# A two-block fp32 kernel: the weights' low halves leave GpSimd, three branch products move in front of the mLSTM norms, a wide norm takes its bank from the product banks

## The chip, the cores and the metric

The kernel runs on one core of one Trainium2 chip. The time is the device time of one execution in microseconds (us). Three runs of the kernel before took 1544.9, 1547.41 and 1548.17 us; their median is 1547.41 us. The engines are named as in the profile: PE does matmuls (PEld its weight loads), DVE is the vector engine, ACT the scalar engine, POOL GpSimd, and SP issues most of the DMAs. Each engine works through its own instructions in their order.

## The reference, cut to what matters

Two transformer-like blocks follow each other over 512 positions of width 1024, all in float32. The first adds 16 meta tokens, so it works on 528 positions.

```
first block
  h = rmsnorm(x);  proj = h @ w_in  -> u, q, k, v, o, gates, ga, gb
  y_a = gelu(ssm(u)) * sigmoid(... @ w_glu)                 # state space branch
  hb  = mlstm(q, k, v, gates)                                # 4 heads of 128
  y_b = hb * rsqrt(mean(hb*hb)) * g_head * sigmoid(o)        # a norm for each head
  merged = sigmoid(ga) * (y_a @ w_a) + sigmoid(gb) * (y_b @ w_b)
  x = x + rmsnorm(merged @ w_out)                            # "post norm"
  x = x + rmsnorm((gelu(conv(h @ w_gate)) * (h @ w_up)) @ w_down)
second block
  x = x + (four head groups A, B, C, D, each its own attention, group norm) @ w_out_2
  x = x + cross_attention(x, 256 memory tokens)
  x = x + relu(h @ w_up_2)**2 @ w_down_2
  return rmsnorm(x)
```

## The kernel before, in words

Activations lie with features on the 128 partitions and positions along the free dimension. To reach float32 accuracy every operand of a product is split in two: a high half (the value rounded to PE's fast float32 form) and a low half (what is left). A product is then three matmuls for each block of 128 features: high by high, high by low, low by high (`mm3`, lines 130 to 138; `product`, lines 150 to 175).

Weights come through `weights` (lines 112 to 128): a DMA by SP into a staging tile `wst`, a cast to the high half `whi` (line 125 on ACT, or line 123 on DVE), and a subtraction for the low half `wlo` (line 126). Each of the three tiles has three buffers. The engine of line 126 is `self.wlow`. It is DVE in most of the kernel. It is POOL from the time that the second block's attention begins until the end of the cross attention (set around the `weave` in `hybrid`, and in `cross`). While it is POOL, every second high half is cast on DVE instead of ACT.

The accumulation banks come from pools. `product_bank` (lines 177 to 189) hands out a bank for a product: where a pool `pmx` of three more banks is open, `mm` (two buffers) and `mx` (three) take turns; where it is not and `third` is set, every third product uses the single bank `rs`; otherwise only the two `mm` banks are used. The row norms use the bank `rs`: `rstd_wide` (lines 249 to 266) sums squares with a matmul by ones (line 257), takes Ln and Exp on ACT (lines 260, 261) and refines on DVE (lines 263 to 266; line 264 is the last to read the bank). `rstd_steps` uses `rs` twice, for column sums (line 279) and for spreading the result (line 294).

The stages that the change touches, in order of time in the trace:

- the end of the mLSTM, about 330 to 350 us: the last head's units, then Ln and Exp of the row scales `rows` on ACT (lines 853 and 854, each with a table load), then matmuls by an identity column that spread `rows` over partitions (line 858, bank `st`), a multiply (line 861) and the split of y_b.
- the merge, about 338 to 400 us: `branch(f, 0)` multiplies y_a by its weights and `branch(f, 1)` y_b by its own; f runs over 8 blocks. The first three `branch(f, 0)` stand first in the code, behind the mLSTM norms.
- the output product and the post norms, about 400 to 475 us: 8 products for each of two halves of the positions, then `post_norm` for each half. The second half's norm runs beside the products of memory keys and values (`memory_keys`, lines 1565 to 1608) and the first products of the feed forward part. No `pmx` is open there, so these products share the two `mm` banks.
- the attention of the second block, about 865 to 1100 us: softmax or stick-breaking steps of one head (DVE, ACT, POOL, PE in turns) woven with the projections of the next.
- the cross attention, about 1100 to 1200 us.

The order of the instructions on each engine is not that of the code: a scheduler reorders the program with a model of its own. So a change of engines also moves instructions.

Of the kernel before, what the change touches and what calls it, by code (L numbers as in the profile page):

```python
# [11 lines left out]
FT = mybir.dt.float32  # L12
FR = mybir.dt.float32r
AF = mybir.ActivationFunctionType
OP = mybir.AluOpType
# [4 lines left out]
P = 128  # L20
DM = 1024
KT = DM // P
# [3 lines left out]
T0 = NM - 2  # L26
# [37 lines left out]
class Net:  # L64
    def __init__(self, ctx, tc, I, out, dump=None):
# [13 lines left out]
        self.wlow, self.turns = nc.vector, 0  # L79
# [32 lines left out]
    def weights(self, src, shape, own=None):  # L112

        nc = self.nc
        kt, cols = shape
        n = kt * cols
        st = self.wst.tile([P, 1024], FT, name="wst")
        nc.sync.dma_start(st[:, 0:n] if len(src.shape) == 2 else st[:, 0:n].rearrange("p (k c) -> p k c", k=src.shape[1]),
                          src)
        hi, lo = ((own or self.whi).tile([P, 1024], FR, name="whi"), (own or self.wlo).tile([P, 1024], FR, name="wlo"))  # L120
        self.turns += 1
        if self.wlow is nc.gpsimd and self.turns % 2:
            nc.vector.tensor_copy(hi[:, 0:n], st[:, 0:n])
        else:
            nc.scalar.activation(hi[:, 0:n], st[:, 0:n], AF.Copy)  # L125
        self.wlow.tensor_tensor(lo[:, 0:n], st[:, 0:n], hi[:, 0:n].bitcast(FT), OP.subtract)  # L126
        v = lambda t: t[:, 0:n].rearrange("p (k c) -> p k c", k=kt)
        return v(hi), v(lo)
# [120 lines left out]
    def rstd_wide(self, out, accs, t, width=DM, bank=None):  # L249
# [6 lines left out]
        for j, acc in enumerate(accs):  # L256
            mm = nc.tensor.matmul(ps, self.ones, acc, start=j == 0, stop=j == len(accs) - 1)
            if bank is not None and j == 0:
                self.tc.keep_in_program_order(mm)
# [447 lines left out]
    def mixer(self):  # L707
# [3 lines left out]
        with ExitStack() as es:  # L711
# [23 lines left out]
            with ExitStack() as e2:  # L735
# [4 lines left out]
                with tc.tile_pool(name="tmp0", bufs=1, side="right", reuse_waits="tile") as tmp:  # L740
# [33 lines left out]
                    for (t0, n) in FULL:  # L774
                        known = self.rstd_wide(rs[:, t0:t0 + n], [a[:, t0:t0 + n] for a in self.nacc],
                                               tmp.tile([P, 264], FT, name=f"rw{t0}"),
                                               bank=self.ptr.tile([P, 512], FT, name="tr"))
# [33 lines left out]
            with ExitStack() as e2:  # L811
# [40 lines left out]
                row = self.rows[:, T0:L]  # L852
                nc.scalar.activation(row, row, AF.Ln, scale=1.0 / P)
                nc.scalar.activation(row, row, AF.Exp, scale=-0.5)
                for h in range(4):
# [13 lines left out]
            jobs = self.merge(self.pool(es, "memp"), mt, yas, ybs, sga, gb, sgs, a2, b2)  # L869
# [36 lines left out]
    def merge(self, mem, mt, yas, ybs, sga, gb, sgs, a2, b2):  # L906
# [3 lines left out]
        mg = []  # L910
# [3 lines left out]
        def branch(f, i):  # L914

            if f not in ws:
                ws[f] = self.weights(I["w_ab"][f], (8, P))
# [3 lines left out]
            for (t0, n) in TAIL:  # L921
# [9 lines left out]
        for f, i in [(0, 0), (1, 0), (2, 0), (0, 1)] + [  # L931
                fi for f in range(1, KT) for fi in ((f, 1), (f + 2, 0)) if fi[0] < KT]:
            branch(f, i)
# [8 lines left out]
        for i, (t0, n) in enumerate(TAIL):  # L942
# [10 lines left out]
            steps = self.post_norm(mt, [y[:, t0 - T0:t0 - T0 + n] for y in yo], accs, t0, n, "g_ffn_pre")  # L953
# [52 lines left out]
    def post_norm(self, pool, ys, accs, t0, n, gnext):  # L1006
# [3 lines left out]
        self.rstd_wide(pr, accs, pool.tile([P, 258], FT, name="prt"))  # L1010
# [298 lines left out]
    def hybrid(self):  # L1309
# [3 lines left out]
        with ExitStack() as es:  # L1313
# [221 lines left out]
            self.wlow = nc.gpsimd  # L1535
            self.vx = self.pool(e2, "vx", 1)
            self.weave([(heads(*hs), expand(jobs)) for hs, jobs in plan[1:]])
            self.wlow = V
# [79 lines left out]
    def cross(self, es, out):  # L1618
# [13 lines left out]
        self.wlow = nc.gpsimd  # L1632
# [95 lines left out]
        self.wlow = V  # L1728
# [213 lines left out]
```

## Time and profile before

| what | value |
|---|---|
| median of three runs | 1547.41 us |
| the profiled execution | 1552.2 us, its span 1550.5 us |
| PE busy | 1474.9 us (95%) |
| DVE busy | 1027.4 us (66%) |
| ACT busy | 728.2 us (47%) |
| POOL busy | 329.9 us (21%) |
| mean granted TensorE clock | 0.989 |

The span runs from the first to the last instruction. A matmul's row shows when it started and a modelled end; matmuls overlap. The idle time of PE is what a change on the other engines can win. In the rows below, a bracket such as [1.69 <-DVE ptl L107] says that the engine stood idle for 1.69 us before this instruction and that a DVE instruction of line 107 ended the wait.

### The profile page before, as it was taken

To read this page: it belongs to the slowest core of one execution; us is meant where nothing else is said; L and a number is where in the kernel's file an instruction comes from. 1 tells how busy PE (TensorE), PEld (TensorE's weight loads), DVE (VectorE), ACT (ScalarE), POOL (GpSimd) and SP (SyncE) were. 2 spreads that over 40 slices of the span, in tenths; PEclk is the share of its full clock that TensorE was granted. 3 is DMA by queue.
4 is the path that set the end of the run, shared out by engine and by line. 5 is a ranking of instruction groups with operands and counts; after the bars stand their busy time and mean duration, and the time that the engine had idled before them with its cause. 6 is when DMAs were issued, how large, how long until landed. Compare 5 with 4: busy or idle time off the path is not lost.

```text
span 1550.5 us, 25022 instructions
## 1 busy us (share of the span) xinstructions
PE 1474.9 (95%) x9769; PEld 1326.8 (86%) x9769; DVE 1027.4 (66%) x1946; ACT 728.2 (47%) x1420; POOL 329.9 (21%) x304
## 2 busy tenths in 40 slices
PE   7999899989989999999999999989789999999996
PEld 7899899879988899999999877878788888888886
DVE  6988889777587555555476778888886443344334
ACT  5323356664655333334454556575565431134322
POOL 1157821003341000000142354303432000000001
PEclk9999999999999999999999999999999999999999
DMA  6333332226553232324656122114221233333221
GB/s 204 98 110 94 111 105 77 73 96 194 161 157 116 96 93 92 91 94 139 187 170 199 55 68 69 48 41 144 84 67 42 95 96 95 95 96 95 92 85 55
DMA packets 66431, 161.97 MB, mean 104 GB/s; under 512 B 15100, under 2 KB 24556, under 8 KB 66184
## 3 DMA queue, kind: packets, MB, share of 16 engines
q1 hardware_dynamic: 64936, 157.74, 33.0%
q8 instruction: 77, 1.26, 0.3%
q0 software_dynamic: 288, 1.57, 0.3%
q10 hardware_dynamic: 1088, 1.05, 0.2%
q14 instruction: 42, 0.34, 0.1%
HBM read 153.92 MB, written 10.33 MB: 106 GB/s over the span
## 4 chain that ended last, share of the span: by engine, by line
PE 55%; DVE 10%; ACT 3%; issue 1%; POOL 0%; ACTq 0%; DVEq 0%; POOLq 0%
PE mm L135 6%; PE mm L138 6%; PE mm L136 6%; PE mm L165 5%; PE mm L168 5%; PE mm L167 5%; PE mx L165 4%; PE mx L168 4%; PE mx L167 4%; DVE xl L110 2%; PE mx L135 2%; PE mx L138 2%; PE mx L136 2%; DVE ptl L107 1%; PE tr L1219 1%
## 5 line engine op out<-in xcount | busy, mean ns | idle before, releaser
L126 DVE TENSOR_TENSOR wlo<-wst,whi 128x1024 fp32r<-128x1024 f32 (+2 forms) x227 | 284.4, 1254 | 200.0 <-ACT whi L125 121.5
L125 ACT ACTIVATE whi<-wst 128x1024 fp32r<-128x1024 f32 (+3 forms) x244 | 251.9, 1033 | 290.0 <-PE mm L136 107.5
L167 PE MATMUL mm<-xh,whi 128*128 128x256 f32 (+4 forms) x792 | 228.7, 314 | 2.5 <-DVE u L751 2.3
L168 PE MATMUL mm<-xl,whi 128*128 128x256 f32 (+4 forms) x792 | 229.3, 314 | 0.3 <-DVE xl L110 0.3
L167 PE MATMUL mx<-xh,whi 128*128 128x512 f32 (+3 forms) x584 | 176.5, 324 | 7.5 <-ACT xh L109 6.8
L168 PE MATMUL mx<-xl,whi 128*128 128x512 f32 (+3 forms) x584 | 177.6, 326 | 3.3 <-DVE xl L110 3.2
L167 PEld LDWEIGHTS mm<-xh,whi 128*128 128x128 f32 (+1 forms) x792 | 149.8, 189 | 12.9 <-DVE u L751 2.6
L168 PEld LDWEIGHTS mm<-xl,whi 128*128 128x128 f32 (+1 forms) x792 | 149.7, 189 | 10.6 <-issue 0.6
L135 PE MATMUL mm<-hh,whi 128*128 128x256 f32 (+1 forms) x496 | 139.9, 311 | 0.0
L136 PE MATMUL mm<-hl,whi 128*128 128x256 f32 (+1 forms) x496 | 139.7, 311 | 0.0
L165 PE MATMUL mm<-xh,wlo 128*128 128x256 f32 (+4 forms) x792 | 137.6, 313 | 0.0
L167 PEld LDWEIGHTS mx<-xh,whi 128*128 128x128 f32 x584 | 110.5, 189 | 16.7 <-ACT xh L109 7.1
L165 PEld LDWEIGHTS mm<-xh,wlo 128*128 128x128 f32 (+1 forms) x792 | 114.6, 188 | 10.3 <-issue 0.4
L168 PEld LDWEIGHTS mx<-xl,whi 128*128 128x128 f32 x584 | 110.3, 189 | 14.3 <-DVE xl L110 5.0
L165 PE MATMUL mx<-xh,wlo 128*128 128x512 f32 (+3 forms) x584 | 105.9, 322 | 0.0
L126 POOL TENSOR_TENSOR wlo<-wst,whi 128x1024 fp32r<-128x1024 f32 (+1 forms) x34 | 75.2, 2215 | 124.1 <-PE mm L138 39.8
L135 PEld LDWEIGHTS mm<-hh,whi 128*128 128x128 f32 x496 | 93.5, 189 | 6.2
L136 PEld LDWEIGHTS mm<-hl,whi 128*128 128x128 f32 x496 | 93.6, 189 | 5.8
L1004 POOL TENSOR_TENSOR acc<-acc,osq 128x256 f32<-128x256 f32 (+1 forms) x26 | 24.8, 954 | 345.4 <-ACT osq L1001 345.3
L165 PEld LDWEIGHTS mx<-xh,wlo 128*128 128x128 f32 x584 | 87.1, 187 | 9.1
L138 PE MATMUL mm<-hh,wlo 128*128 128x256 f32 (+1 forms) x496 | 83.9, 310 | 1.3 <-DVE wlo L126 1.3
L138 PEld LDWEIGHTS mm<-hh,wlo 128*128 128x128 f32 x496 | 70.8, 189 | 7.4 <-DVE wlo L126 1.7
(555 smaller groups left out, 3317.3 us busy)
## 6 DMA issues: line engine op xcount, KB each, us to landing
wst<-in_w_in_dram SPq DMA_DIRECT2D x52, 512.0 KB, 3.5
wst<-in_w_down_dram SPq DMA_DIRECT2D x32, 512.0 KB, 3.5
wst<-in_w_mup_dram SPq DMA_DIRECT2D x32, 512.0 KB, 3.5
wst<-in_w_mdown_dram SPq DMA_DIRECT2D x32, 512.0 KB, 3.8
wst<-in_w_gate_dram SPq DMA_DIRECT2D x22, 512.0 KB, 3.5
wst<-in_w_up_dram SPq DMA_DIRECT2D x22, 512.0 KB, 3.5
wst<-in_w_out_dram SPq DMA_DIRECT2D x20, 512.0 KB, 3.6
wst<-in_w_down_dram SPq DMA_DIRECT2D x16, 384.0 KB, 3.6
```

Of the source, the lines that this page charges most:

```text
L107: nc.vector.tensor_tensor(lo, src, hi.bitcast(FT), OP.subtract)
L110: nc.vector.scalar_tensor_tensor(lo, src, gain, hi.bitcast(FT), OP.mult, OP.subtract)
L125: nc.scalar.activation(hi[:, 0:n], st[:, 0:n], AF.Copy)
L126: self.wlow.tensor_tensor(lo[:, 0:n], st[:, 0:n], hi[:, 0:n].bitcast(FT), OP.subtract)
L135: nc.tensor.matmul(ps, ah, bh, start=start and i == 0, stop=False)
L136: nc.tensor.matmul(ps, ah, bl, start=False, stop=False)
L138: nc.tensor.matmul(ps, al, bh, start=False, stop=stop and i == n - 1)
L165: nc.tensor.matmul(ps, wl[:, k], xh, start=False, stop=k == KT - 1)
L167: nc.tensor.matmul(ps, wh[:, k], xh, start=k == 0, stop=False)
L168: nc.tensor.matmul(ps, wh[:, k], xl, start=False, stop=False)
L1004: nc.gpsimd.tensor_tensor(acc, acc, sq, OP.add)
L1219: nc.tensor.matmul(yp[0:64, c0:c1], m[:, j, vc:vc + 64], d[:, j - f0, c0:c1], start=ji == x == 0, stop=ji == len(jobs) - 1 and x == 2)
```

## The change

1. `weights` loses the choice of engine: all high halves are cast by ACT, all low halves are subtracted by DVE, in the attention and the cross attention as elsewhere.
2. `branch` and the loading of its weights become functions of their own, `branches`. The weights of f = 0, 1, 2 and the products `branch(f, 0)` of these three are now written ahead of and behind the Ln and Exp of `rows`, in front of the spreading matmuls, while the mLSTM's own banks are still open and `pmx` is not. So these six products (three f, two ranges) use `mm` and `rs` in turns.
3. `post_norm` in the merge takes its bank from `product_bank` instead of `rs`. That also shifts which of `mm` and `mx` the later products get. A flag `late` keeps the fixed place of the first norm of the program as it was.

```
@@ -76,7 +76,6 @@
         self.nrm = ent("nrm")
         self.dram = ent("dram", 1, DR)
         self.pmx, self.turn, self.third = None, 0, 0
-        self.wlow, self.turns = nc.vector, 0
         self.pmm = ent("pmm", 2, PS)
 
         c = self.const
@@ -118,12 +117,8 @@
         nc.sync.dma_start(st[:, 0:n] if len(src.shape) == 2 else st[:, 0:n].rearrange("p (k c) -> p k c", k=src.shape[1]),
                           src)
         hi, lo = ((own or self.whi).tile([P, 1024], FR, name="whi"), (own or self.wlo).tile([P, 1024], FR, name="wlo"))
-        self.turns += 1
-        if self.wlow is nc.gpsimd and self.turns % 2:
-            nc.vector.tensor_copy(hi[:, 0:n], st[:, 0:n])
-        else:
-            nc.scalar.activation(hi[:, 0:n], st[:, 0:n], AF.Copy)
-        self.wlow.tensor_tensor(lo[:, 0:n], st[:, 0:n], hi[:, 0:n].bitcast(FT), OP.subtract)
+        nc.scalar.activation(hi[:, 0:n], st[:, 0:n], AF.Copy)
+        nc.vector.tensor_tensor(lo[:, 0:n], st[:, 0:n], hi[:, 0:n].bitcast(FT), OP.subtract)
         v = lambda t: t[:, 0:n].rearrange("p (k c) -> p k c", k=kt)
         return v(hi), v(lo)
 
@@ -246,7 +241,7 @@
             pass
         return self.r
 
-    def rstd_wide(self, out, accs, t, width=DM, bank=None):
+    def rstd_wide(self, out, accs, t, width=DM, bank=None, late=False):
 
 
         nc = self.nc
@@ -255,7 +250,7 @@
         ps = (self.pmm.tile([P, 512], FT, name="rs", bufs=1) if bank is None else bank)[:, 0:n]
         for j, acc in enumerate(accs):
             mm = nc.tensor.matmul(ps, self.ones, acc, start=j == 0, stop=j == len(accs) - 1)
-            if bank is not None and j == 0:
+            if late and j == 0:
                 self.tc.keep_in_program_order(mm)
         nc.scalar.activation(out, ps, AF.Ln, scale=1.0 / width, bias=self.eps)
         nc.scalar.activation(out, out, AF.Exp, scale=-0.5)
@@ -774,7 +769,7 @@
                     for (t0, n) in FULL:
                         known = self.rstd_wide(rs[:, t0:t0 + n], [a[:, t0:t0 + n] for a in self.nacc],
                                                tmp.tile([P, 264], FT, name=f"rw{t0}"),
-                                               bank=self.ptr.tile([P, 512], FT, name="tr"))
+                                               bank=self.ptr.tile([P, 512], FT, name="tr"), late=True)
                     for i, piece in enumerate(pieces):
                         if i not in early:
                             piece()
@@ -850,8 +845,15 @@
                 self.weave([(units, fill)])
 
                 row = self.rows[:, T0:L]
+                mg = []
+                load, branch = self.branches(mg, sga, gb, a2, b2)
+                for f in range(3):
+                    load(f)
                 nc.scalar.activation(row, row, AF.Ln, scale=1.0 / P)
                 nc.scalar.activation(row, row, AF.Exp, scale=-0.5)
+
+                for f in range(3):
+                    branch(f, 0)
                 for h in range(4):
                     for (t0, n) in TAIL:
                         ps = self.pst.tile([P, 512], FT, name="st")[:, 0:n]
@@ -866,7 +868,9 @@
                     self.dump("yb", h, ybs[h])
             self.third = 0
             self.pmx = self.pool(es, "pmx2", 3, PS)
-            jobs = self.merge(self.pool(es, "memp"), mt, yas, ybs, sga, gb, sgs, a2, b2)
+            for f, i in [(0, 1)] + [fi for f in range(1, KT) for fi in ((f, 1), (f + 2, 0)) if fi[0] < KT]:
+                branch(f, i)
+            jobs = self.merge(self.pool(es, "memp"), mt, yas, ybs, mg, sgs)
         self.ffn(*jobs)
 
     def pool(self, es, name, bufs=1, space=None, side=None):
@@ -903,18 +907,18 @@
         return pre, [(lambda i=i: load(i), [lambda f=f, r=r: part(f, *r) for f in (2 * i, 2 * i + 1) for r in TAIL])
                      for i in range(2)]
 
-    def merge(self, mem, mt, yas, ybs, sga, gb, sgs, a2, b2):
+    def branches(self, mg, sga, gb, a2, b2):
+
         nc = self.nc
         V = nc.vector
         I = self.I
-        mg = []
         free = [8, 9, 10, 11, 12, 13, 14, 15, 0, 1, 2, 3, 4, 5, 6, 7]
         ws = {}
 
         def branch(f, i):
 
             if f not in ws:
-                ws[f] = self.weights(I["w_ab"][f], (8, P))
+                load(f)
             wh, wl = ws[f]
             if i:
                 mg.append([self.ring.tile([P, L], FR, name=f"r{j}") for j in free[2 * f:2 * f + 2]])
@@ -927,10 +931,14 @@
                 if i:
                     nc.gpsimd.tensor_tensor(gs[0], gs[0], gs[1], OP.add)
                     self.split(mg[f][0][:, t0:t0 + n], mg[f][1][:, t0:t0 + n], gs[0], 0.5)
-
-        for f, i in [(0, 0), (1, 0), (2, 0), (0, 1)] + [
-                fi for f in range(1, KT) for fi in ((f, 1), (f + 2, 0)) if fi[0] < KT]:
-            branch(f, i)
+        def load(f):
+            ws[f] = self.weights(I["w_ab"][f], (8, P))
+        return load, branch
+
+    def merge(self, mem, mt, yas, ybs, mg, sgs):
+        nc = self.nc
+        V = nc.vector
+        I = self.I
         self.xp = self.pool(self.ctx, "xp", side="right")
         self.load_x(self.xp, I["x"], [nc.sync])
         self.bias_rows(mt)
@@ -950,7 +958,8 @@
                 next(steps, None)
             for _ in steps:
                 pass
-            steps = self.post_norm(mt, [y[:, t0 - T0:t0 - T0 + n] for y in yo], accs, t0, n, "g_ffn_pre")
+            steps = self.post_norm(mt, [y[:, t0 - T0:t0 - T0 + n] for y in yo], accs, t0, n, "g_ffn_pre",
+                                   self.product_bank)
 
         e2 = ExitStack()
         jobs = self.ffn_jobs(e2)
@@ -1003,11 +1012,11 @@
                 return [acc, sq]
             nc.gpsimd.tensor_tensor(acc, acc, sq, OP.add)
 
-    def post_norm(self, pool, ys, accs, t0, n, gnext):
+    def post_norm(self, pool, ys, accs, t0, n, gnext, bank=None):
 
         V = self.nc.vector
         pr = pool.tile([P, 258], FT, name="prs")[:, 0:n]
-        self.rstd_wide(pr, accs, pool.tile([P, 258], FT, name="prt"))
+        self.rstd_wide(pr, accs, pool.tile([P, 258], FT, name="prt"), bank=bank and bank())
         yield
         for k in range(KT):
             x = self.x[k][:, t0:t0 + n]
@@ -1532,10 +1541,8 @@
             e3.close()
             self.at = self.pool(e2, "at", 6)
             self.ap = self.pool(e2, "ap", 1)
-            self.wlow = nc.gpsimd
             self.vx = self.pool(e2, "vx", 1)
             self.weave([(heads(*hs), expand(jobs)) for hs, jobs in plan[1:]])
-            self.wlow = V
             if self.dump:
                 for n in range(KT):
                     self.dump("y" + "ABCD"[n // 2], n % 2, ys[n])
...
```

The two left-out places only set `self.wlow` back and forth around the cross attention, as the fragment at line 1532 does for the attention.

How the scheduler then orders the engines is seen at three places. `order` rows name line, operation, and output<-inputs; the numbers behind the names tell tiles of one name apart.

On DVE in the stick-breaking steps of head group B (`pth`, `ptl` are the high and low halves of the score tile `e`; `qkn` is a normalised projection of the next head), before:

```order
L1266 CAST pth0_10695<-e_10649 128x128
L1259 TENSOR_SCALAR e_10703<-tr_10606 128x128
L1267 TENSOR_TENSOR ptl0_10696<-e_10649,pth0_10695 128x128
L1248 SCALAR_TENSOR_TENSOR e_10660<-sc_10657,e_10660 128x384
L123 CAST whi_11293<-wst_11291 128x1024
L107 TENSOR_TENSOR ptl1_10540<-e_10660,pth1_10539 128x384
L1365 SCALAR_TENSOR_TENSOR qkn_10938<-mm_11099,rs_8436 128x512
```

The same place after the change:

```order
L1275 CAST pth0_10695<-e_10649 128x128
L1276 TENSOR_TENSOR ptl0_10696<-e_10649,pth0_10695 128x128
L1257 SCALAR_TENSOR_TENSOR e_10660<-sc_10657,e_10660 128x384
L1374 SCALAR_TENSOR_TENSOR qkn_10938<-mm_11099,rs_8436 128x512
L121 TENSOR_TENSOR wlo_11294<-wst_11291,whi_11293 128x1024
L1257 SCALAR_TENSOR_TENSOR e_10715<-tr_10712,e_10715 128x512
L106 TENSOR_TENSOR ptl1_10540<-e_10660,pth1_10539 128x384
```

The cast of `whi_11293` has gone to ACT. Its low half, which POOL subtracted, stands on DVE as `wlo_11294`, ahead of `ptl1_10540`.

On PE at the end of the mLSTM (the `wlo` rows end a `branch(f, 0)` product; line 858 of before, 860 of after, spreads `rows`), before, where three such products (banks `mm_4505`, `mm_4539`, `mm_4573`) stand ahead of the spreading:

```order
L138 MATMUL mm_4573<-xh0_4180,wlo_4556 128x256
L138 MATMUL mm_4573<-xh1_4182,wlo_4556 128x256
L138 MATMUL mm_4573<-xh2_4184,wlo_4556 128x256
L138 MATMUL mm_4573<-xh3_4186,wlo_4556 128x256
L858 MATMUL st_4432<-rows_104,ident_78 128x258
L858 MATMUL st_4437<-rows_104,ident_78 128x256
```

After:

```order
L131 MATMUL rs_4506<-xl3_4187,whi_4444 128x258
L133 MATMUL rs_4506<-xh0_4180,wlo_4445 128x258
L133 MATMUL rs_4506<-xh1_4182,wlo_4445 128x258
L133 MATMUL rs_4506<-xh2_4184,wlo_4445 128x258
L133 MATMUL rs_4506<-xh3_4186,wlo_4445 128x258
L133 MATMUL mm_4520<-xh3_4186,wlo_4445 128x256
L1118 MATMUL rs_5073<-ya0_5068,rel_5066 12x320
L860 MATMUL st_4534<-rows_104,ident_78 128x258
L860 MATMUL st_4539<-rows_104,ident_78 128x256
```

Six products stand ahead of the spreading now (`mm_4450`, `rs_4464`, `mm_4478`, `mm_4492`, `mm_4520`, `rs_4506`). The three with 258 or 256 columns that have moved came behind the spreading matmuls before.

On PE at the second post norm (line 257 of before, 252 of after, sums the squares; `ya` and `yb` are the high and low halves of the memory tokens; `mm_6007` and `mm_5870` are products of memory values or keys), before:

```order
L138 MATMUL mm_6007<-whi_5918,yb0_5153 128x256 x2
L138 MATMUL mm_6007<-whi_5918,yb1_5200 128x256 x2
L138 MATMUL mm_6007<-whi_5924,yb2_5251 128x256
L257 MATMUL rs_5844<-acc_5473,ones_83 128x256
L257 MATMUL rs_5844<-osq_5833,ones_83 128x256
L138 MATMUL mm_6007<-whi_5924,yb2_5251 128x256
L138 MATMUL mm_6007<-whi_5924,yb3_5302 128x256 x2
L167 MATMUL mm_6043<-xh0_5087,whi_5969 128x258
```

After:

```order
L133 MATMUL mm_5870<-ya0_5152,wlo_5856 128x256 x2
L133 MATMUL mm_5870<-ya1_5199,wlo_5856 128x256 x2
L274 MATMUL rs_5712<-ones_83,nacc_5103 86x1 x3
L252 MATMUL mm_5844<-osq_5833,ones_83 128x256
L133 MATMUL mm_5870<-ya2_5250,wlo_5856 128x256 x2
L133 MATMUL mm_5870<-ya3_5301,wlo_5856 128x256 x2
L130 MATMUL mm_5928<-ya0_5152,whi_5866 128x256
```

The norm's matmul has moved forward by three products of the memory tokens, and it fills `mm_5844`, one of the two `mm` banks, where it filled `rs_5844`.

## Rows read from the trace of the kernel before

**Rows 1.** Windows over attention and cross attention: each engine's busy us (x instructions)

```profile
core 0: us, PE busy (x) PEld busy (x) DVE busy (x) ACT busy (x) POOL busy (x), PEclk, DMA share, GB/s
...
sum 340.00, PE 312.08 PEld 275.53 DVE 274.37 ACT 207.03 POOL 118.35; mean PE 104.03 PEld 91.84 DVE 91.46 ACT 69.01 POOL 39.45
```

**Rows 2.** Waits of PE, 860 to 1200 us: total us, times, longest

```profile
PE mm L135 <- DVE x L1652: 3.8, 3, 1.9
...
PE mm L167 <- DVE x L1652: 0.2, 1, 0.2
```

**Rows 3.** Groups by shape on POOL: count, busy us, mean ns, idle before

```profile
L126 POOL TENSOR_TENSOR wlo<-wst,whi 128x1024 fp32r<-128x1024 f32 x26 | 64.3, 2478 | 63.0 <-PE tr L1219 25.4 <-ACT whi L125 15.7 <-PE mm L1360 6.3
...
L126 POOL TENSOR_TENSOR wlo<-wst,whi 128x512 fp32r<-128x512 f32 x8 | 10.8, 1360 | 61.1 <-PE mm L138 37.6 <-PE mm L1360 9.1 <-DVE qs L1131 7.1
```

**Rows 4.** Groups by shape on DVE, the whole span

```profile
L126 DVE TENSOR_TENSOR wlo<-wst,whi 128x1024 fp32r<-128x1024 f32 x210 | 268.4, 1279 | 188.5 <-ACT whi L125 110.1 <-PE mx L165 35.7 <-PE mm L165 33.5
...
L123 DVE CAST whi<-wst 128x1024 fp32r<-128x1024 f32 x13 | 12.7, 974 | 2.4 <-PE mm L136 1.2 <-issue 1.2
...
L107 DVE TENSOR_TENSOR ptl<-tr,pth 128x384 fp32r<-128x384 f32 x8 | 4.4, 548 | 0.0
...
L107 DVE TENSOR_TENSOR ptl<-e,pth 128x384 fp32r<-128x384 f32 x4 | 4.2, 1059 | 2.2 <-ACT pth L106 2.2
...
L123 DVE CAST whi<-wst 128x512 fp32r<-128x512 f32 x4 | 1.7, 422 | 0.0
```

**Rows 5.** Groups by shape on ACT, 860 to 1200 us

```profile
L125 ACT ACTIVATE whi<-wst 128x1024 fp32r<-128x1024 f32 x19 | 19.8, 1053 | 5.3 <-PE mm L138 3.6 <-PE mm L136 0.9 <-PE mm L1363 0.4
...
L125 ACT ACTIVATE whi<-wst 128x512 fp32r<-128x512 f32 x4 | 2.5, 629 | 2.7 <-POOL wlo L126 2.7
```

**Rows 6.** Timeline at 919 to 923 us: start, duration, instruction [idle before]

```profile
919.46 2.35 POOL L126 TENSOR_TENSOR wlo<-wst,whi 128x1024 fp32r<-128x1024 f32 x1
...
919.66 2.57 DVE L107 TENSOR_TENSOR ptl<-e,pth 128x384 fp32r<-128x384 f32 x1 [0.91 <-ACT pth L106]
...
922.28 0.44 PE L1256 MATMUL sc<-ptl,ntri 128*128 128x384 f32 x1 [1.69 <-DVE ptl L107]
```

**Rows 7.** Chain of waits, 860 to 1200 us: start, length, step

```profile
873.97 2.34 DVE kl L1144
...
1120.61 2.32 DVE xl L110
```

**Rows 8.** Windows of five stretches at a low granted clock

```profile
860.70:864.20 3.50, 3.50 (x19) 3.50 (x19) 1.10 (x2) 1.93 (x2) 0.00 (x0) 0.51 0.00 0
...
1079.20:1086.00 6.80, 6.43 (x32) 5.72 (x30) 4.85 (x26) 5.09 (x19) 0.00 (x0) 0.50 0.42 149
...
sum 20.60, PE 20.23 PEld 19.03 DVE 12.04 ACT 11.33 POOL 2.16; mean PE 4.05 PEld 3.81 DVE 2.41 ACT 2.27 POOL 0.43
```

**Rows 9.** Timeline of PE at the mLSTM's end

```profile
341.86 2.35 PE L858 MATMUL st<-rows,ident 128*128 128x258 f32 x8 [1.67 <-ACT rows L854]
...
349.25 0.28 PE L135 MATMUL mx<-xh,whi 128*128 128x258 f32 x1
...
350.68 0.28 PE L135 MATMUL mx<-xh,whi 128*128 128x258 f32 x1
...
360.41 0.39 PE L135 MATMUL mx<-xh,whi 128*128 128x258 f32 x1 [2.38 <-ACT whi L125]
```

**Rows 10.** Timeline at the second post norm, and a window behind it

```profile
447.82 0.39 PE L135 MATMUL mm<-ya,whi 128*128 128x256 f32 x1 [1.15 <-ACT osq L1001]
...
456.75 0.59 PE L257 MATMUL rs<-acc,ones 128*128 128x256 f32 x2
...
461.45 0.41 DVE L264 SCALAR_TENSOR_TENSOR prt<-rs,prt 128x256 f32<-128x256 f32 x1
...
470.03 0.39 PE L168 MATMUL mx<-xl,whi 128*128 128x256 f32 x1 [2.58 <-DVE xl L110]
...
471.60:475.00 3.40, 3.31 (x15) 2.97 (x14) 3.40 (x4) 0.99 (x3) 2.96 (x4) 0.50 0.00 0
```

More of the change, by code (lines that the diff above doesn't have):

```diff
@@ L120, in weights @@
         hi, lo = ((own or self.whi).tile([P, 1024], FR, name="whi"), (own or self.wlo).tile([P, 1024], FR, name="wlo"))
[L121 to L126, printed above, removed]
+        nc.scalar.activation(hi[:, 0:n], st[:, 0:n], AF.Copy)
+        nc.vector.tensor_tensor(lo[:, 0:n], st[:, 0:n], hi[:, 0:n].bitcast(FT), OP.subtract)
         v = lambda t: t[:, 0:n].rearrange("p (k c) -> p k c", k=kt)
@@ L247, in rstd, with rstd_wide @@
         return self.r
-    def rstd_wide(self, out, accs, t, width=DM, bank=None):
+    def rstd_wide(self, out, accs, t, width=DM, bank=None, late=False):
         nc = self.nc
@@ L257, in rstd_wide @@
             mm = nc.tensor.matmul(ps, self.ones, acc, start=j == 0, stop=j == len(accs) - 1)
-            if bank is not None and j == 0:
+            if late and j == 0:
                 self.tc.keep_in_program_order(mm)
@@ L776, in mixer @@
                                                tmp.tile([P, 264], FT, name=f"rw{t0}"),
-                                               bank=self.ptr.tile([P, 512], FT, name="tr"))
+                                               bank=self.ptr.tile([P, 512], FT, name="tr"), late=True)
                     for i, piece in enumerate(pieces):
@@ L852, in mixer @@
                 row = self.rows[:, T0:L]
+                mg = []
+                load, branch = self.branches(mg, sga, gb, a2, b2)
+                for f in range(3):
+                    load(f)
                 nc.scalar.activation(row, row, AF.Ln, scale=1.0 / P)
                 nc.scalar.activation(row, row, AF.Exp, scale=-0.5)
+                for f in range(3):
+                    branch(f, 0)
                 for h in range(4):
@@ L868, in mixer @@
             self.pmx = self.pool(es, "pmx2", 3, PS)
-            jobs = self.merge(self.pool(es, "memp"), mt, yas, ybs, sga, gb, sgs, a2, b2)
+            for f, i in [(0, 1)] + [fi for f in range(1, KT) for fi in ((f, 1), (f + 2, 0)) if fi[0] < KT]:
+                branch(f, i)
+            jobs = self.merge(self.pool(es, "memp"), mt, yas, ybs, mg, sgs)
         self.ffn(*jobs)
@@ L916, in branch @@
             if f not in ws:
-                ws[f] = self.weights(I["w_ab"][f], (8, P))
+                load(f)
             wh, wl = ws[f]
@@ L929, in branch, with load, merge @@
                     self.split(mg[f][0][:, t0:t0 + n], mg[f][1][:, t0:t0 + n], gs[0], 0.5)
-        for f, i in [(0, 0), (1, 0), (2, 0), (0, 1)] + [
-                fi for f in range(1, KT) for fi in ((f, 1), (f + 2, 0)) if fi[0] < KT]:
-            branch(f, i)
+        def load(f):
+            ws[f] = self.weights(I["w_ab"][f], (8, P))
+        return load, branch
+    def merge(self, mem, mt, yas, ybs, mg, sgs):
+        nc = self.nc
+        V = nc.vector
+        I = self.I
         self.xp = self.pool(self.ctx, "xp", side="right")
@@ L952, in merge @@
                 pass
-            steps = self.post_norm(mt, [y[:, t0 - T0:t0 - T0 + n] for y in yo], accs, t0, n, "g_ffn_pre")
+            steps = self.post_norm(mt, [y[:, t0 - T0:t0 - T0 + n] for y in yo], accs, t0, n, "g_ffn_pre",
+                                   self.product_bank)
         e2 = ExitStack()
@@ L1004, in out_tile, with post_norm @@
             nc.gpsimd.tensor_tensor(acc, acc, sq, OP.add)
[L1006 removed]
+    def post_norm(self, pool, ys, accs, t0, n, gnext, bank=None):
         V = self.nc.vector
         pr = pool.tile([P, 258], FT, name="prs")[:, 0:n]
[L1010 removed]
+        self.rstd_wide(pr, accs, pool.tile([P, 258], FT, name="prt"), bank=bank and bank())
         yield
```

8 lines of the change are left out of this document (1 added, 7 removed).

## The prediction

> **What bounds the kernel now.** I read the busy times first: PE is busy 95% of the span, so the change can win PE's idle time, PE's time at the lower clock, and nothing else. Then I read windows over the stage that the first edit changes. In the 340 us of attention and cross attention PE is busy 312.1 us [rows 1], so it idles 27.9, far more than its share elsewhere; DVE is busy 274.4 us (81%), ACT 207.0, POOL 118.4. The waits of PE there come next: 16 rows end with a DVE instruction, from 3.8 us down to 0.2 (the first and the last are shown [rows 2]), and add up to 21.7 us; seven end with ACT, 6.4. So in this stage the releaser that is late is DVE, and the question is why.
>
> The groups by shape answer it. On DVE the same subtraction of 128x384 takes 548 ns where one operand is a bank (`tr`) and 1059 where both lie in the on-chip memory (`e`, `pth`) [rows 4]. The timeline shows one of the slow ones: POOL starts a low half of weights at 919.46 for 2.35 us, DVE starts `ptl` at 919.66 and ends at 922.23, 0.42 behind POOL's end; the matmul that wants it stood 1.69 us [rows 6]. The chain of waits shows that such instructions are on the path: eight single DVE steps over 2 us (first and last [rows 7]), 20.3 us together.
>
> The Trainium skill has a rule for this (SBUF — State Buffer, "SBUF: two separate sides"): DVE with two inputs from that memory and GpSimd reading it exclude each other, one blocks until the other is done. The trace agrees: the 2.57 us are POOL's rest of 2.15 and 0.42 of work. By the rule the whole surplus goes with the low halves, which is the rival "more comes back" below.
>
> **First edit: weights.** POOL loses 26 low halves of 128x1024 and 8 of 128x512, 64.3 + 10.8 = 75.1 us [rows 3]. DVE gets them: 26 x 1.279 = 33.3, and 8 of 128x512, for which I halve the 1.279, 5.1, together 38.4 [rows 4]. It loses its casts, 12.7 + 1.7 = 14.4 [rows 4]. And it loses the stretch. If each of the 34 low halves stretched one DVE instruction by half of POOL's mean of 75.1/34 = 2.2 us, that is 34 x 1.1 = 37; the bounds are 0 (none met) and 75 (each met in full). I take 37 as an estimate: 38.4 - 14.4 - 37 = -13, so DVE becomes a little less busy. ACT gets 13 x 1.053 + 4 x 0.629 = 16.2 us [rows 5] on 207 of 340.
>
> On the path: the eight long steps would have taken some 0.6 each (`ptl<-tr` 0.55 [rows 4]), so they hold 20.3 - 4.8 = 15.5 us of surplus, and with three long steps more of the same chain (a pair of `xl`, a `wlo`, a pair of `e`), about 18. Not all returns, since the order shows a low half of 1.28 us put on DVE ahead of `ptl1_10540`: where a stretch of 2.0 leaves, 1.28 may stand in its place, and 0.7 is left. Elsewhere the low half falls where DVE idles (66 us of 340) and all of it returns. Halfway between these is about 9. The ends are 0, where each low half lands in front of a waited-for step, and 18. ACT's 16.2 us are hidden by its 133 idle us, save where PE idles: charged at PE's idle share of 8% they cost 1.3. Net -7.7.
>
> The clock belongs to this. PE ran five stretches there at a granted clock of about 0.5, 1.2 instead of 2.4 GHz, 20.6 us together; the longest is 1079.2 to 1086.0 [rows 8]. Full speed would give back at most half, 10.3. The first, 860.7 to 864.2 [rows 8], has no low half of POOL beside it and stays. Before the other four PE had waited a little, and a quarter fewer of these gives a quarter of (20.6 - 3.5)/2 = 8.6, -2 (ends 0 and -8.6; a new wait can also cause one, +1.7 for a stretch of 3.4).
>
> **Second edit: branch products in front of the norms.** Before, PE stood 1.67 us until Exp of `rows` was there [rows 9]. Three more products now stand ahead of the spreading. One takes 350.68 - 349.25 = 1.43 us [rows 9], so 4.3 of work moves forward: 1.67 of it fills the wait and 2.6 delays the norms' chain (spread, multiply, split of y_b). Behind it the same three products are missing as cover, and `branch(f, 1)` is wanted 2.6 + 1.67 us earlier relative to it. I take -1.2 for the filled wait. The next hole, 2.38 us for a cast at 360.41 [rows 9], waits for a weight buffer held by the first products; they end earlier now, and half of it goes, -1.2. The ends are -4 (both holes) and +1.5 (the y_b chain is bare by the length of one product). The three loads on SP keep their order and ACT issues the same instructions, so neither queue costs anything. -2.4.
>
> **Third edit: the bank of the wide norms.** The second norm's matmul no longer stands behind three products of the memory tokens; it moves from 456.75 to about 448, where the first of these starts [rows 10]. So `x` of the feed-forward part comes earlier, and the 2.58 us hole at 470.03 and the half-speed stretch behind it, 3.4 us, 1.7 lost, can go: -4.3 [rows 10]. Against it, the norm now holds one of only two product banks from its matmul to line 264, in before from 456.75 to 461.86, 5.1 us [rows 10]. In that time memory products have one bank, and each waits for its reader: one product of 1.43 is covered, so up to +3.7 is not. Both mechanisms have rows and neither is nearer; I take +0.5, leaning on the wait because it comes first. The first norm takes a bank while five are open and costs nothing; if that cover failed, one product, 1.4.
>
> **Sum.** -7.7 - 2 - 2.4 + 0.5 = -11.6. The profiled execution took 1552.2, so 1540.6 as profiled; the median of the runs lies 4.8 below it, so 1535.8, rounded to 1536.
>
> **The rivals.**
> *More comes back.* The stretch leaves whole and the low halves fall into DVE's idle time: -18 +1.3, half of the clock (-4.3), the two other edits as above: -22.9, 1524.5. For it: rows 6 show blocking in full. Against it: the order places low halves ahead of waited-for steps.
>
> *DVE refills it.* Where DVE is the late engine, 38.4 us of new work cost on it what the stretch cost. Nothing comes back in the attention (0, +1.3, clock 0), and the small edits leave -1.9 between them: -0.6, 1546.8. For it: DVE is 81% busy; in favour of before, POOL had room (118 of 340). Against it: 14.4 us of casts leave DVE too. The Trainium skill states a rule on that side (Perfetto Trace Analysis, "Optimizing Scalar/DVE Operations"): a saturated DVE is a reason to give work to ScalarE or GpSimd, though the shared port may spoil the latter. Whether 81% is saturated, no row tells.
>
> *Slower: ACT's queue.* Every high half is now a cast on ACT, which must wait for PE to release a `whi` buffer; the exponentials, splits and copies of the attention stand behind it. The 23 casts there waited 8.0 us, 0.35 each [rows 5]. Seventeen more are 16.2 + 6 = 22 us, and with DVE's gain refilled as above, a share s of it on the path gives -1.9 + 22 s. It decides from s = 0.3: +4.7, 1552; at one half 1556. For it: ACT already ends 6.4 us of PE's waits. Against it: the low halves that held the `whi` buffers for 2.5 us on POOL now take 1.3.
>
> *Bank.* The third edit costs its +3.7 and the rest is as forecast: -8.4, 1539, inside the forecast's own range.
>
> **How the numbers follow.** About 0.2% (3.1 us) is what a measurement of this kernel can tell from no change. Forecast, its own range 1530 to 1542: 0.53. More comes back: 0.10. DVE refills: 0.20, of which 0.06 faster, 0.10 same, 0.04 slower by that bound. ACT's queue: 0.17, of which 0.04 same, 0.13 slower. So faster 0.69, same 0.14, slower 0.17. The range 1526 to 1550 leaves out part of the second case and most of the last, about 2 in 10; I choose 1536.
>
> **What would show it.** Right: no 128x1024 low half on POOL; `ptl<-e` of 128x384 near 0.55 to 0.7 us and DVE's busy time in the attention at or under its old one; PE's idle time from 860 to 1200 under 22 us; no wait ahead of the spreading matmuls; the norm's matmul at about 448 and no hole at 470. Wrong: DVE's busy time up by 20 us with the waits still ended by it (refill); waits of PE for `pth`, `e` or `whi` by ACT above 12 us (ACT's queue); a wait of a memory product for line 264 above 3 us (bank). If `ptl<-e` stays slow without POOL beside it, the reading of rows 6 falls and with it the largest term.

## The result, and the profile after

The changed kernel took 1536.66 us (median of five runs, 1533.36 to 1538.99) against 1548.17 us for the kernel before (five runs, 1544.9 to 1554.06). The ratio on record, which goes by all the runs, is 0.991, 95% interval 0.988 to 0.994; that of the two medians is 0.993. The forecast was 1536 us, with a range from 1526 to 1550. A second set of five runs on another occasion gave 1536.18 us and 0.991 (0.990 to 0.992). The profiled execution's span fell from 1550.5 to 1537.3 us, by 13.2.

Where the time went is found by counting PE's matmuls, of which both programs have 9769, and comparing when the same number starts. The 2200th starts 2.5 us later than before (298.8 against 296.3), the 2800th 1.1 later (383.7, 382.6), the 3600th 0.8 later (488.8, 488.0), the 6200th 0.9 later (852.9, 852.0), the 7600th 4.7 earlier (1091.7, 1096.4) and the 8400th 12.5 earlier (1218.1, 1230.6). So 13.4 us came from the attention and the cross attention, 1.4 from the end of the mLSTM, 0.3 from the post norms. Some 2.5 us were lost ahead of all three, in a part that the change does not touch.

Windows over the two attention stages, which end at about 1187 us now (the columns are those of [rows 1]):

```profile
860.00:975.00 115.00, 111.90 (x666) 99.71 (x665) 80.99 (x167) 74.69 (x160) 17.46 (x33) 0.96 0.20 65
975.00:1100.00 125.00, 116.20 (x757) 100.64 (x755) 103.60 (x331) 89.19 (x247) 1.57 (x2) 0.97 0.24 76
1100.00:1187.00 87.00, 81.15 (x597) 74.04 (x598) 71.52 (x185) 57.15 (x158) 23.48 (x29) 1.00 0.24 80
sum 327.00, PE 309.25 PEld 274.39 DVE 256.11 ACT 221.03 POOL 42.51; mean PE 103.08 PEld 91.46 DVE 85.37 ACT 73.68 POOL 14.17
```

PE idles 17.8 us of 327 where it idled 27.9 of 340 [rows 1]. DVE has all the low halves and is yet 18 us less busy over these stages; ACT has 14 us more. The waits of PE from 860 to 1188 us:

```profile
PE tr L1228 <- DVE ptl L106: 3.1, 3, 1.2
PE tr L1228 <- ACT pth L105: 2.1, 3, 1.3
PE sc L1182 <- DVE nm L1187: 1.9, 4, 0.8
...
PE tr L1283 <- DVE pth L1275: 1.4, 1, 1.4
PE mm L130 <- DVE x L1658: 1.1, 2, 0.7
...
PE tr L1204 <- DVE e L1200: 0.2, 1, 0.2
```

All rows that end with DVE add up to 10.5 us (21.7 before [rows 2]), those with ACT to 6.1 (6.4 before). The groups by shape on DVE there, answering to [rows 4]:

```profile
L121 DVE TENSOR_TENSOR wlo<-wst,whi 128x1024 fp32r<-128x1024 f32 x31 | 37.9, 1227 | 6.2 <-ACT whi L120 4.0 <-ACT hh L105 1.1 <-PE mm L1369 0.9
...
L1140 DVE TENSOR_TENSOR qs<-qkn,qs 64x512 fp32r<-64x512 f32 x16 | 11.1, 696 | 1.1 <-ACT qs L1139 0.5
...
L121 DVE TENSOR_TENSOR wlo<-wst,whi 128x512 fp32r<-128x512 f32 x8 | 5.5, 685 | 3.4 <-issue 2.5 <-PE mm L1369 0.8
...
L106 DVE TENSOR_TENSOR ptl<-e,pth 128x384 fp32r<-128x384 f32 x4 | 2.2, 553 | 1.3 <-ACT pth L105 1.3
```

`ptl<-e` of 128x384 takes 553 ns, as the form with one operand in a bank did before (548), where it took 1059 [rows 4]. The queries' split `qs<-qkn,qs` fell from 817 ns to 696; before:

```profile
L1131 DVE TENSOR_TENSOR qs<-qkn,qs 64x512 fp32r<-64x512 f32 x16 | 13.1, 817 | 1.1 <-ACT qs L1130 0.6
```

The chain of waits holds no single DVE step over 2 us in this stage any more (before, the eight of the prediction [rows 7] and a `wlo` of 2.52); its longest DVE piece is a pair:

```profile
1097.71 2.27 DVE wlo L121 x2
```

The clock is the other part of the picture. Half-speed stretches (the granted clock is the third number from the end) between 861 and 1077 us:

```profile
861.00:864.80 3.80, 3.60 (x18) 3.60 (x19) 1.30 (x4) 1.52 (x2) 0.00 (x0) 0.57 0.00 0
957.00:963.90 6.90, 6.18 (x29) 6.18 (x30) 4.32 (x8) 2.43 (x6) 1.37 (x3) 0.51 0.05 16
1018.30:1021.80 3.50, 3.50 (x21) 3.29 (x20) 3.37 (x13) 2.20 (x7) 0.00 (x0) 0.53 0.04 5
1073.30:1076.80 3.50, 3.21 (x18) 3.05 (x18) 2.60 (x15) 2.65 (x12) 0.00 (x0) 0.54 0.37 121
```

Summed as one minus the granted clock over each microsecond, they lose 8.5 us against 10.2 [rows 8]. Ahead of 860 us it went the other way: 8.5 us lost in four places against 3.4 in two. The largest is a stretch that only one of the two traces has, behind the same short wait (1.48 us at 188.11 after, 1.50 at 187.89 before). After, and then the same 7.1 us before:

```profile
188.40:195.50 7.10, 7.10 (x38) 7.10 (x38) 2.34 (x4) 2.06 (x5) 4.74 (x5) 0.55 0.37 114
```

```profile
187.90:195.00 7.10, 7.10 (x61) 7.10 (x62) 4.81 (x11) 2.49 (x6) 5.05 (x5) 1.00 0.43 114
```

38 matmuls where there were 61. Over this stretch the lag behind the kernel before grew from 0.2 to 3.4 us, and by the 1500th matmul it was back at the 2.5 lost ahead of the change.

PE at the end of the mLSTM, and at the second post norm:

```profile
348.04 0.70 PE L1118 MATMUL rs<-ya,rel 32*12 32x320 f32 x2 [0.40 <-DVE sga L930]
349.01 1.13 PE L860 MATMUL st<-rows,ident 128*128 128x258 f32 x4 [0.27 <-ACT rows L853]
...
445.05 1.22 PE L252 MATMUL mm<-acc,ones 128*128 128x256 f32 x2 [0.50 <-POOL acc L1013]
...
449.94 0.68 PE L252 MATMUL mm<-osq,ones 128*128 128x256 f32 x2
451.61 0.39 PE L130 MATMUL mm<-ya,whi 128*128 128x256 f32 x1 [0.52 <-DVE rst L281]
...
462.63 0.38 PE L162 MATMUL mm<-xh,whi 128*128 128x258 f32 x1 [1.52 <-DVE vl L109]
```

The 1.67 us ahead of the spreading matmuls have become 0.27, and the 2.38 us hole behind them is gone [rows 9]. The norm's matmuls start at 445.05 and 449.94, where they started at 456.75 [rows 10] and 457.19, and the 2.58 us hole at 470 is gone [rows 10]; in its place the first product of the feed-forward part waits 1.52 us for DVE, which is still reading memory values from an `mm` bank. All of PE's waits from 400 to 480 us add up to 6.2 us, against 6.7 before.

### The profile page after: what moved, and what is told of

It reads as the page before. It is cut to its first block, busy times and chain, and to the rows that moved or that the text cites. A ratio compares the mean times of both kernels' runs of the same rounds, so it can differ in the third digit from the quotient of the medians.

```text
span 1537.3 us, 25021 instructions
## 1 busy us (share of the span) xinstructions
PE 1476.9 (96%) x9769; PEld 1331.7 (87%) x9769; DVE 1004.7 (65%) x1963; ACT 742.8 (48%) x1437; POOL 256.3 (17%) x270
## 4 chain that ended last, share of the span: by engine, by line
PE 65%; DVE 7%; ACT 2%; DMA 2%; issue 1%; SPq 0%; POOL 0%; DVEq 0%; ACTq 0%; POOLq 0%
PE mm L130 6%; PE mm L133 6%; PE mm L131 6%; PE mm L160 5%; PE mm L163 5%; PE mm L162 5%; PE mx L160 4%; PE mx L163 4%; PE mx L162 4%; PE mx L130 3%; PE mx L131 3%; PE mx L133 2%; PE mm L1371 2%; PE mm L1372 2%; PE mm L1369 2%; PE tr L1228 1%
## 5 line engine op out<-in xcount | busy, mean ns | idle before, releaser
L121 DVE TENSOR_TENSOR wlo<-wst,whi 128x1024 fp32r<-128x1024 f32 (+2 forms) x261 | 320.1, 1228 | 200.1 <-ACT whi L120 120.7
L120 ACT ACTIVATE whi<-wst 128x1024 fp32r<-128x1024 f32 (+2 forms) x261 | 267.9, 1028 | 295.7 <-PE mm L131 113.2
L163 PEld LDWEIGHTS mm<-xl,whi 128*128 128x128 f32 (+1 forms) x800 | 151.1, 189 | 10.5 <-issue 0.6
L130 PE MATMUL mm<-hh,whi 128*128 128x256 f32 (+1 forms) x480 | 133.4, 308 | 0.0
L131 PE MATMUL mm<-hl,whi 128*128 128x256 f32 (+1 forms) x480 | 133.3, 308 | 0.0
L236 POOL TENSOR_TENSOR nacc<-nacc,sq 128x256 f32<-128x256 f32 (+2 forms) x58 | 55.6, 960 | 208.3 <-ACT sq L235 199.1
L133 PE MATMUL mm<-hh,wlo 128*128 128x256 f32 (+1 forms) x480 | 80.0, 308 | 1.3 <-DVE wlo L121 1.3
```

Of the source, the lines that this page charges most:

```text
L121: nc.vector.tensor_tensor(lo[:, 0:n], st[:, 0:n], hi[:, 0:n].bitcast(FT), OP.subtract)
L130: nc.tensor.matmul(ps, ah, bh, start=start and i == 0, stop=False)
L131: nc.tensor.matmul(ps, ah, bl, start=False, stop=False)
L133: nc.tensor.matmul(ps, al, bh, start=False, stop=stop and i == n - 1)
L163: nc.tensor.matmul(ps, wh[:, k], xl, start=False, stop=False)
L236: (nc.vector if k % len(accs) else nc.gpsimd).tensor_tensor(acc[:, c:c + w], acc[:, c:c + w], sq, OP.add)
```

## The experiments

Each was compared with the kernel before on the same chip. The kernel before had a median there of 1550.78 us beside `weights_only`, `branch_and_bank` and the two runs that take lows and casts apart, of 1548.91 beside `pool_reads`, `pool_memsets`, `sums_on_dve` and `after_again`, and of 1549.68 beside the others. An expectation in us goes by the 1548 us of the first result, so it is best read against the ratio. Two theories stood against each other for the first edit. The port theory: low halves on GpSimd stretch (make longer) DVE's instructions that run beside them and read two operands from the on-chip memory. The cast theory: the 17 casts taken off DVE are what relieves it. The second and the third edit were to be separated as well.

**The first edit alone, and the other two alone.** `weights_only` has the new `weights` in the kernel before; `branch_and_bank` is the changed kernel with the old `weights`; `bank_only` adds only this, with the argument passed on down to `rstd_wide`, to the kernel before (shortened):

```
-            steps = self.post_norm(mt, [...], accs, t0, n, "g_ffn_pre")
+            steps = self.post_norm(mt, [...], accs, t0, n, "g_ffn_pre", self.product_bank)
```

> The first edit alone. Port theory: the time from 860 to 1200 us falls by 11 to 14 us as in the changed kernel; total 1535 to 1540 us. If the three edits help each other, less than 8 us comes back and the total is 1541 us or more.

Measured: 1538.04 us, ratio 0.992 (0.991 to 0.994). The first edit alone gives 12 of the 13 us. In its trace the stretch from the 6200th to the 8400th matmul is 12.7 us shorter than before, as the port theory expected.

> The second and the third edit alone; the weights as before. By the two traces compared, the products in front of the norms are worth about 3 us and the bank 0 to 1: 1544 to 1546 us, the time from 330 to 385 us shorter by 3, that from 860 to 1200 us unchanged within 2. Rival (both edits only move a wait): 1548 us, no difference at 385 us.

Measured: 1547.81 us, ratio 0.998 (0.997 to 0.999): 3 us less than the kernel before took beside it, as forecast, and not the rival's "no difference". In the trace the stretch from the 2200th to the 2800th matmul is 3.1 us shorter. That from the 6200th to the 8400th is 2.8 shorter, where 2 were allowed; it lost 3.4 us less to the clock than before, which accounts for that.

> The third edit alone: the wide norms of the merge take their banks from the product banks; weights and branch as before. The prediction had +0.5 us for it (from -4.3 to +3.7); the traces compared say -0.3: ratio 0.998 to 1.001, so that the -3 us of branch_and_bank are the second edit's. Rival: the bank brings the -3 us, ratio 0.998 or less, and no hole of 2.5 us is left at 470 us.

Measured: 1551.17 us, ratio 1.001 (0.999 to 1.002). The bank alone is not told from nothing, so the 3 us of `branch_and_bank` lie with the branch products; no run has these alone. The traces agree: from the 2200th to the 2800th matmul, less the time lost to the clock there, the eleven profiled kernels with the second edit take 82.9 to 84.1 us and the three without it (`before`, `weights_only`, `bank_only`) 85.4 to 86.3. The 2.58 us hole is gone here too (its place shows waits of 1.6 and 0.7), and still nothing is won.

**Lows and casts apart.** `lows_dve_casts_mixed` and `lows_pool_casts_act` are the changed kernel with one half of the first edit undone (shortened):

```
lows_dve_casts_mixed
+        if <in the attentions> and self.turns % 2: nc.vector.tensor_copy(hi, st)      # every second cast on DVE
lows_pool_casts_act
-        nc.vector.tensor_tensor(lo, st, hi, OP.subtract)
+        self.wlow.tensor_tensor(lo, st, hi, OP.subtract)                              # GpSimd in the attentions
```

> The changed kernel, but every second high half in the attention and the cross attention is still cast on DVE, as before; the low halves are all on DVE. Port theory (GpSimd's low halves stretch DVE's two-input steps, and that is what the first edit takes away): the stretch is gone, ptl<-e of 128x384 near 0.55 us, and the time from 860 to 1200 us falls by 8 to 13 us against before although DVE has 14.4 us more to do than in the changed kernel; total 1537 to 1541 us. Cast theory (the 17 casts that leave DVE are what relieves it): the gain of the attention is gone, total 1546 us or more.

Measured: 1535.54 us, ratio 0.990 (0.988 to 0.991): all of the gain, with the casts where they were, and a little more than the expectation had. `ptl<-e` of 128x384 took 655 ns, between the 553 of the changed kernel and the 1059 of before. The traces leave one thing open. From the 6200th to the 8400th matmul, less the time lost to the clock, this kernel takes 360.4 us and the changed kernel 356.6; but it lost 3.4 us to the clock there and the changed kernel 8.5. So the casts on DVE may cost some 4 us that the clock gave back; with one trace of it that is not shown.

> The changed kernel, but the low halves of the attention and the cross attention are on GpSimd as before; all high halves are cast on ACT. Port theory: ptl<-e of 128x384 stays near 1.06 us, and most of the first edit's gain is missing; total 1543 to 1549 us. Cast theory: DVE is relieved of 14.4 us, total 1536 to 1540 us.

Measured: 1546.96 us, ratio 0.997 (0.996 to 0.998), against 0.998 for `branch_and_bank`, which differs only in the casts. So moving the casts brings nothing that the intervals tell apart, and the cast theory falls. One detail of the expectation missed: `ptl<-e` of 128x384 does not stay slow. The scheduler puts the low halves beside other steps, and these are slow instead:

```profile
L1141 DVE TENSOR_TENSOR qs<-qkn,qs 64x512 fp32r<-64x512 f32 x16 | 16.1, 1005 | 3.5 <-ACT qs L1140 3.1
...
L1277 DVE TENSOR_TENSOR ptl<-e,pth 128x512 fp32r<-128x512 f32 x4 | 4.5, 1123 | 0.1
...
L107 DVE TENSOR_TENSOR ptl<-e,pth 128x384 fp32r<-128x384 f32 x4 | 2.4, 595 | 2.2 <-ACT pth L106 2.1
```

**GpSimd made busy again, without any work changing hands.** These are the changed kernel with idle work added behind each pair of halves in the two attentions (shortened); nobody reads the scratch tile `t`:

```
pool_reads             +  for each 205 columns c: nc.gpsimd.tensor_tensor(t, st[c], hi[c], OP.subtract)
pool_memsets           +  for each 205 columns:   nc.gpsimd.memset(t, 0.0)
pool_reads_constants   +  for each 205 columns:   nc.gpsimd.tensor_tensor(t, self.ones, self.ident, OP.subtract)
pool_memsets_long      +  three times as many memsets
```

> The changed kernel, and GpSimd also subtracts the same halves (four pieces of 205 columns for a 128x1024) into a scratch tile that nobody reads; no work of DVE or ACT differs. Port theory: GpSimd's reads stretch DVE's two-input steps again; 5 to 10 us come back on the span, total 1542 to 1548 us, and DVE's busy time from 860 to 1200 us grows by 20 us or more. Rival (GpSimd's low halves cost nothing to DVE, their late results did): no change against the changed kernel, 1535 to 1539 us.

Measured: 1551.14 us, ratio 1.001 (1.000 to 1.003): 15 us slower than the changed kernel, more than expected. DVE's busy time from 860 to 1200 us is 276.6 us against 262.6 in the profile of `after_again`, 14 more and not 20; but as this kernel is slower, less of the work lies in that window. From the 6200th to the 8400th matmul DVE is busy 302.3 us against 278.5, 24 more. That stretch takes 17 us longer in the trace, and 7 of these are lost to the clock (15.4 us against 8.5).

> As pool_reads, but GpSimd sets the scratch tile to zero instead, so it is busy at the same places and reads nothing. Port theory in the form that the reading by GpSimd is what blocks: within 3 us of the changed kernel, 1535 to 1540 us, and DVE's busy time as there. Rivals: any GpSimd work blocks DVE, or GpSimd's queue delays its own masks: as slow as pool_reads, 1542 to 1548 us.

Measured: 1535.63 us, ratio 0.991 (0.990 to 0.992), as the changed kernel. But these memsets kept GpSimd busy for 30 us only. Hence two more:

> As pool_memsets with three times as many pieces, some 90 us of GpSimd time, as much as in pool_reads. Port theory: no DVE instruction is stretched, and only GpSimd's own masks of the stick-breaking heads come later: within 4 us of the changed kernel, 1534 to 1541 us. Rival (GpSimd's queue): 1544 us or more.

Measured: 1533.35 us, ratio 0.990 (0.987 to 0.992). 93 us of GpSimd time that reads nothing cost nothing that shows in the total.

> As pool_reads, but GpSimd subtracts two constant tiles of 128 columns at the same places, so it holds no buffer of the weights; 120 such pieces of about 0.53 us. Port theory: the reading alone stretches DVE, 5 to 12 us against the changed kernel, total 1541 to 1549 us. Rival (pool_reads was slow because its subtractions kept the weights' buffers busy): within 3 us of the changed kernel, 1533 to 1539 us.

Measured: 1539.1 us, ratio 0.993 (0.991 to 0.995). The total is 6 us above `pool_memsets_long`, whose runs all lie below all of these, and between the two expectations. The groups of the idle work and of one DVE step that reads two operands, from 860 to 1200 us, in `pool_reads`, `pool_reads_constants` and `pool_memsets_long`:

```profile
L126 POOL TENSOR_TENSOR idle<-wst,whi 128x205 f32<-128x205 f32 x120 | 107.5, 896 | 111.4 <-issue 67.5 <-PE tr L1233 21.9 <-ACT whi L121 13.8
...
L1145 DVE TENSOR_TENSOR qs<-qkn,qs 64x512 fp32r<-64x512 f32 x16 | 14.2, 890 | 1.0 <-ACT qs L1144 0.4
```

```profile
L126 POOL TENSOR_TENSOR idle<-ones,ident 128x128 f32<-128x128 f32 x115 | 71.6, 622 | 110.9 <-PE tr L1233 103.9
...
L1145 DVE TENSOR_TENSOR qs<-qkn,qs 64x512 fp32r<-64x512 f32 x16 | 12.0, 753 | 2.6 <-ACT qs L1144 2.1
```

```profile
L126 POOL MEMSET idle<- 128x205 f32 x335 | 92.8, 277 | 123.6 <-PE tr L1233 106.9
...
L1145 DVE TENSOR_TENSOR qs<-qkn,qs 64x512 fp32r<-64x512 f32 x16 | 11.1, 695 | 0.6 <-ACT qs L1144 0.2
```

890, 753 and 695 ns, beside 696 in the changed kernel: GpSimd instructions that read slow this step, in the order of their amount, and memsets do not. That is the port theory. But the constants cost 3 us against `after_again` (by intervals that overlap; 6 against `pool_memsets_long`) for 72 us of reading, and `pool_reads` 15 for 108; its subtractions also keep the weights' tiles in use for longer. How much of the 15 us is that, how much the worse place of the reads, and how much the clock, stays open.

The traces show more than the theory says: DVE steps with one operand are stretched too. In the kernel before, a cast of 128x1024 took 0.69 us at 1098.28, and the next one of the same shape 2.90, beside a low half on GpSimd:

```profile
1099.10 2.53 POOL L126 TENSOR_TENSOR wlo<-wst,whi 128x1024 fp32r<-128x1024 f32 x1 [22.40 <-PE tr L1219]
...
1099.27 2.90 DVE L123 CAST whi<-wst 128x1024 fp32r<-128x1024 f32 x1
```

And the cast `kl<-kl` of 64x512 took 601 ns on average before and 432 in the changed kernel; it took 540 in `pool_reads`, 500 in `pool_reads_constants` and 490 in `pool_memsets_long`. In the last of these, two casts beside memsets alone took 0.52 us (867.01) and 0.55 (868.78), so for casts memsets may count a little as well.

**What is left on GpSimd.** In the attentions the changed kernel still has sums of squares (`nacc`, 0.84 us each) and the triangular masks of the stick-breaking heads on GpSimd. `sums_on_dve` moves the sums, `sums_and_masks_on_dve` the masks too (`G.tensor_tensor(e, e, self.strict, ...)` becomes `V.tensor_tensor`). `after_again` is the changed kernel beside them.

> The changed kernel, and the sums of squares (nacc) in the attention and the cross attention go from GpSimd to DVE. Port theory: 34 sums of 0.84 us on GpSimd become 34 of 0.41 us on DVE (14 us), and the stretch that they cause beside the xl steps of the cross attention (about 9 us of DVE) goes: total 1533 to 1537 us. Rival (DVE's load decides): slower than the changed kernel by 2 us or more.

Measured: 1533.94 us, ratio 0.991 (0.989 to 0.992).

> The changed kernel itself, to stand beside the runs of this chip: 0.991 of the kernel before. If the earlier difference to lows_dve_casts_mixed (0.990) was scatter, 0.990 to 0.992.

Measured: 1536.18 us, ratio 0.991 (0.990 to 0.992).

> sums_on_dve, and the 32 triangular masks of the stick-breaking heads go from GpSimd (0.53 us each) to DVE as well, so GpSimd reads nothing during the attention. Port theory: DVE gains 32 x 0.28 = 9 us of work and loses what is left of the stretch (6 us), and the masks' results come 0.25 us sooner each: 1531 to 1536 us. Rival (DVE's load decides): 1537 us or more.

Measured: 1532.75 us, ratio 0.989 (0.986 to 0.991). Both are on the expected side, and DVE's load decides in neither. But the intervals overlap that of the changed kernel, and `pool_memsets_long`, which adds only useless work, came out at 0.990: differences of 2 us between these variants are not told apart. No version is shown to beat the changed kernel.

## Why the prediction was right

The total was met within a microsecond of the median, partly by errors that cancel: in the traces the first edit won 4 us more than forecast, and 2.5 us were lost ahead of the change, which no term had. By the ratio of all runs the gain is 13.6 us where 11.6 were forecast. Three pieces of the chain of before, which the prediction names without their lengths:

```profile
1103.94 4.14 DVE xl L110 x2
...
1140.60 2.52 DVE wlo L126
...
1147.01 2.73 DVE e L1191 x2
```

By the prediction's own steps:

- **Low halves and casts, -7.7 us.** The mechanism was right, the size too small. The attentions gave 13.4 us in the traces, of which 1.7 are clock, so 11.7; `weights_only` gives 12 in all. The -9 was half of "about 18" us of surplus on the chain. That 18 was itself too small. It has 15.5 for eight steps and some 2.5 for three more, but those three are the rows above, and after the change one such `xl` takes 0.61 us, a `wlo` 1.23 and an `e` 0.39 on average, so the three hold about 6, and the long steps about 22 (an estimate from these rows); stretched steps under 2 us were not counted at all. So 11.7 is about half of the long steps' surplus, and no run tells how much of it returned. The step feared, a `wlo` ahead of a waited-for `ptl`, does not show: none stands close ahead of the three waits for `ptl` that are left (3.1 us). Low halves stand ahead of a wait for `pth` (1.4 us at 956.37) and of one for `x` (0.4 at 1100.37). And the +1.3 for ACT did not come: the waits that it ends went from 6.4 to 6.1 us. The unknown price, a 128x512 low half on DVE, was 685 ns against 640 estimated. DVE's busy time was to fall by 13; over the two stages it fell by 18 (274.4 to 256.1), so by the same sum the stretch that left was about 41 and not 37.
- **Clock, -2 us.** In the stage -1.7 in the two traces; as the stretches differ between executions, that is luck as much as reckoning. Ahead of the stage the profiled execution lost 5.1 us more than that of before, which no term had; the half-speed stretches of the part before the change differ from run to run.
- **Branch products, -2.4 us.** The trace shows -1.4 up to the 2800th matmul; a half-speed stretch at 318 to 323 us lies within and costs 1.7, so without it -3.1. The spreading matmuls start 7.1 us later by the clock; 2.5 and 1.7 of these are the clock's, which leaves 2.9, where 2.6 were worked out. The holes of 1.67 and 2.38 us are gone but for 0.67. On the chip 3 us for the second and third edit together. So size and mechanism were about right.
- **Bank, +0.5 us.** -0.3 in the trace and 1.001 (0.999 to 1.002) for it alone. Both mechanisms named are there: the hole at 470 goes, and a bank is waited for. But the waiter was mis-named. No memory product waits for the norm, though the norm holds its bank for 8.9 us (445.05 to 453.90) and not 5.1; the first feed-forward product waits, 1.52 us, for the memory values in the other bank. And the 1.7 us of clock that were to go with the hole did not go: the half-speed stretch of 3.4 us that stood behind the hole at 471.6 [rows 10] stands at 445.1 in the trace after, where the granted clock is 0.50 until 448.5. That the total came out near nothing is two misses that cancel.

The rival "DVE refills it" falls with DVE's busy time and with `sums_and_masks_on_dve`, where DVE gets still more and nothing is lost. "ACT's queue" falls with the 6.1 us, and since `lows_dve_casts_mixed`, which takes the moved casts off ACT again, is not measurably faster. "More comes back" was too high: net of ACT it had 16.7 us for the first edit, the forecast 7.7, and the 11.7 lie between them; its total, 1524.5, was 12 us off.

The rule of the Trainium skill that the prediction drew on (SBUF — State Buffer, "SBUF: two separate sides") is borne out in its form: only a GpSimd instruction that reads stretched DVE's two-operand step (890 and 753 ns), and memsets did not (695). The prediction spoke of steps with two inputs alone; one of its eight long steps, 2.81 us of the chain at 1099.36, is the cast with one input shown above.

## What to carry to other kernels

Work moved to an idle GpSimd is not free: where a DVE step on PE's path, a cast too, is twice as long as the same shape elsewhere, look in the timeline for a GpSimd instruction beside it, and price that instruction by what it does to DVE and not by its own time. Add up the surplus of all stretched steps on the chain, by the time that each form takes undisturbed: here 18 us were counted where the long steps alone held about 22. And before a difference of 2 us in 1540 is explained, sum the half-speed stretches of both traces: ahead of 860 us two executions of the changed kernel lost 8.5 and 5.1 us to them.

## What was not expected of the hardware

The same wait of 1.5 us at 188 us was followed by 7 us at half speed in one trace and by none in the other; in `after_again`, the same program as the first of these, a wait of 1.24 us at that place was followed by none. Over the whole span the sum lost to the clock ran from 11.4 us (`lows_dve_casts_mixed`) to 23.1 (`bank_only`) in single profiled executions, a spread larger than the effect of either of the two smaller edits.
